# Attention in pairs: two 64-feature heads, or two score maps, placed side by side in the halves of the matmul array

## The chip, the core and the metric

The kernel is one program on one core of a Trainium2 chip. Its time is the device time of one execution in microseconds (us); the figure for the kernel before is the median of three runs. Five engines run their own instruction queues: TensorE (PE) multiplies, with a row of its own for the loading of weights (PEld); VectorE (DVE), ScalarE (ACT) and GpSimd (POOL) work on tiles in the on-chip memory; SyncE (SP) issues the transfers.

## What is computed

Two transformer blocks on 256 tokens of 1024 features, in fp32. The parts that matter here are the attentions. In the first block three of them read the same normalised input, and their outputs go through gated branches that are added up:

```python
# MoBA: 8 heads of 64; with 256 tokens and blocks of 256 it is causal attention
s = einsum('bhqd,bhkd->bhqk', q, k) * 64 ** -0.5;  p = softmax(where(causal, s, -inf));  o = p @ v
# FoX: 8 heads of 64; cum is the running sum of a log-forget gate per head
s = einsum('bhqd,bhkd->bhqk', q, k) * scale + cum_q[..., None] - cum_k[None, :];  then as above
# memory: 4 heads of 128 over 256 memory tokens, not causal
```

The second block has a recurrent mixer and, in its second layer, differential attention: 8 heads of 128, each with two score maps of 64 features,

```python
p = masked_softmax(einsum('bhcqd,bhckd->bhcqk', q, k) * 64 ** -0.5, mask)   # c = 0, 1
attn = p[:, :, 0] - lmb * p[:, :, 1];   o = attn @ v
```

followed by a mixture of 8 experts, of which each token uses 2.

## The kernel before

**Dense work.** All large weights come as items of 1 MB (128 x 2048 fp32) through SP's queue into a ring of buffers (class `Stream`, L217). ACT rounds each item to a high part (L307), DVE subtracts it to get the low part (L309), and PE makes each product in three passes, high by high, high by low and low by high (`mm3`, L477, lines 482, 484 or 486, and 491 or 493). `fm_unit` (L537) makes 128 features by 256 tokens with 24 matmuls; `tok_cols` (L552) makes 128 tokens by 512 features with 24.

**Attention beside it.** Attention is cut into steps that wait in a list called `beside`. `tick()` (L518) takes the next one, and the dense functions call it at fixed places: `fm_unit` behind every 24 matmuls, `tok_cols` in the middle and at the end of 24. So PE's program reads: a dense piece, a step of attention, a dense piece, and so on. Instructions in `urgent()` get a higher priority; within these rules a scheduler puts each engine's instructions in order when the program is built. Each engine runs its queue in that order.

**One step** (`attention`, L793). In step i of 11, for 8 heads and LAG = 2, three things stand in a row: `weigh(i-3)` multiplies the transposed probabilities `pt` by the values `v` into a bank `yp` (L822, L823); `turn(i-2)` transposes the three 128 x 128 blocks of P on PE (L808 to L810) and ACT copies them into `pt`; `begin(i)` calls `scores` (L771). There the first query tile, which sees 128 keys, and the second, which sees 256, each get their query by key product (L781), in FoX the bias as one more product (L783), and on the last 128 keys the causal mask, as a product of the identity with a mask in bf16 (L785). Each tile is an accumulation of its own in one bank of PSUM. Then DVE takes the row's maximum (L788), ACT the exponential with its sum (L789), DVE the reciprocal and the scaling (L790, L803).

A head of 64 features uses half of the array: heads 2j and 2j+1 lie on partitions 0 to 63 and 64 to 127 of the same q and k tile (`pair`, L844), so their score products use different rows of the array; in `weigh` they fill different halves of the output columns. Before the change the two heads of a pair come one step apart.

**Three kinds of this attention.** MoBA's steps lie beside the dense work of `branch(yc)` and the projections for FoX; FoX's lie beside `branch(ym)`. FoX needs two more tiles per head, fq and fk, which DVE makes (`fox_bias`, L898). Differential attention has a `begin` of its own (L1253), which calls `scores` once for each map of a head, with banks from the pools `pa` and `pb` (four PSUM banks each), a `turn` (L1266) and a `step` (L1279); it lies beside the projections of the second half of the heads, whose rotation DVE computes. The memory attention (4 heads of 128 features) goes through the same function with one head in a step.

Of the kernel before, what the change touches and what calls it, by code (L numbers as in the profile page):

```python
# [10 lines left out]
F32 = mybir.dt.float32  # L11
F32R = mybir.dt.float32r
# [3 lines left out]
AF = mybir.ActivationFunctionType  # L16
ALU = mybir.AluOpType
AX = mybir.AxisListType
# [3 lines left out]
S = 256  # L22
# [8 lines left out]
LAG, PRIO = 2, 400  # L31
# [319 lines left out]
def tile_kernel(ctx: ExitStack, tc: tile.TileContext, cst, par, wst, x, mem, g_mix, g_mem, g_ffn, w_forget,  # L351
                moe_w_router, ln_g, ln_b, out):
    nc = tc.nc
    V, A, T = nc.vector, nc.scalar, nc.tensor
# [8 lines left out]
    sm = pool("sm", 2)  # L363
# [16 lines left out]
    f1 = c1.enter_context(tc.tile_pool(name="f1", bufs=1))  # L380
# [34 lines left out]
    ident = cs[:, C_ID:C_ID + 128]  # L415
# [46 lines left out]
    def evac_split(hi, lo, ps):  # L462
        A.activation(out=hi, in_=ps, func=AF.Copy)
        V.tensor_tensor(lo, ps, hi.bitcast(F32), op=ALU.subtract)  # L464
# [303 lines left out]
            A.activation(out=v[:, t], in_=ps, func=AF.Copy)  # L768
        return v

    def scores(sp, q, k, causal, bank, bias=None, bufs=3):  # L771


        n0 = 128 if causal else S
        ps = bank("sc")[:, 0:n0 + S]
        P = sp.tile([128, 512], F32, name="P", tag="P", bufs=bufs)[:, 0:n0 + S]
        nmx = sm.tile([128, 2], F32, tag="nmx", name="nmx", bufs=4)
        sums = sm.tile([128, 2], F32, tag="sums", name="sums", bufs=4)
        for t, c in ((0, slice(0, n0)), (1, slice(n0, n0 + S))):
            nk = c.stop - c.start  # L780
            T.matmul(ps[:, c], q[:, t * 128:t * 128 + 128], k[:, 0:nk], start=True, stop=not causal and bias is None)  # L781
            if bias is not None:
                T.matmul(ps[:, c], bias[0][:, t * 128:t * 128 + 128], bias[1][:, 0:nk], start=False, stop=not causal)  # L783
            if causal:
                T.matmul(ps[:, c.stop - 128:c.stop], identb, causb, start=False, stop=True)  # L785
        with urgent():
            for t, c in ((0, slice(0, n0)), (1, slice(n0, n0 + S))):
                V.tensor_reduce(out=nmx[:, t:t + 1], in_=ps[:, c], axis=AX.X, op=ALU.max, negate=True)  # L788
                A.activation(out=P[:, c], in_=ps[:, c], func=AF.Exp, bias=nmx[:, t:t + 1], accum_out=sums[:, t:t + 1])  # L789
            V.reciprocal(out=sums, in_=sums)  # L790
        return P, sums

    def attention(Y, nh, dh, q, k, v, causal, bias=None):  # L793

        hb = 128 // dh
        n0 = 128 if causal else S
        halves = ((0, slice(0, n0)), (1, slice(n0, n0 + S)))
        P, pt, yp = {}, {}, None

        def begin(h):  # L800
            P[h], rs = scores(f1, q(h), k(h), causal, pa, bias(h) if bias is not None else None)
            for t, c in halves:
                V.tensor_scalar(out=P[h][:, c], in0=P[h][:, c], scalar1=rs[:, t:t + 1], scalar2=None, op0=ALU.mult)  # L803

        def turn(h):
            p = P.pop(h)
            pT = pb("pT").rearrange("p (c t) -> p c t", c=4)
            T.transpose(pT[:, 0], p[:, 0:128], ident)  # L808
            T.transpose(pT[:, 1], p[:, n0:n0 + 128], ident)
            T.transpose(pT[:, 2], p[:, n0 + 128:n0 + 256], ident)  # L810
            if not causal:
                T.transpose(pT[:, 3], p[:, 128:256], ident)
            pt[h] = f1.tile([128, 4, 128], F32, tag="pt", name="pt", bufs=2)
            n = 3 if causal else 4
            A.activation(out=pt[h][:, 0:n], in_=pT[:, 0:n], func=AF.Copy)

        def weigh(h, yp):
            r = h % (2 * hb)
            o = yp[(h % hb) * dh:(h % hb) * dh + dh, r // hb]
            hv = slice(h * dh, h * dh + dh)  # L820
            p = pt.pop(h)
            T.matmul(o, v[:, 0, hv], p[:, 0:2], start=True, stop=False)  # L822
            T.matmul(o[:, 128:256], v[:, 1, hv], p[:, 2], start=False, stop=causal)  # L823
            if not causal:
                T.matmul(o[:, 0:128], v[:, 1, hv], p[:, 3], start=False, stop=True)
            if r == 2 * hb - 1:
                b2 = h // hb - 1
                evac_split(Y[0][:, b2:b2 + 2], Y[1][:, b2:b2 + 2], yp)

        def step(i):  # L830
            nonlocal yp
            h = i - LAG - 1
            if h >= 0:
                if h % (2 * hb) == 0:
                    yp = half(pb("yp"))
                weigh(h, yp)
            if 0 <= i - LAG < nh:
                turn(i - LAG)
            if i < nh:
                begin(i)  # L840

        beside.extend(lambda i=i: step(i) for i in range(nh + LAG + 1))

    def pair(t):  # L844
        return lambda h: t[64 * (h % 2):64 * (h % 2) + 64, h // 2]
# [51 lines left out]

    def fox_bias(h):  # L898
        m = C_MISC
        fq = f1.tile([80, S], F32R, name="fq", tag="fq", bufs=1)  # L900
        fk = f1.tile([80, S], F32R, name="fk", tag="fk", bufs=1)
# [351 lines left out]
    def begin(h):  # L1253
        q, k = qk[h // 4]
        b = h % 4
        P0, r0 = scores(da, q[0:64, b], k[0:64, b], True, pa, bufs=4)
        P1, r1 = scores(da, q[64:128, b], k[64:128, b], True, pb, bufs=4)
        with urgent():
            V.tensor_scalar(out=r1, in0=r1, scalar1=nl, scalar2=None, op0=ALU.mult)
            for t, c in ((0, slice(0, 128)), (1, slice(128, 384))):  # L1260
                V.tensor_scalar(out=P1[:, c], in0=P1[:, c], scalar1=r1[:, t:t + 1], scalar2=None, op0=ALU.mult)
                V.scalar_tensor_tensor(out=P0[:, c], in0=P0[:, c], scalar=r0[:, t:t + 1], in1=P1[:, c],
                                       op0=ALU.mult, op1=ALU.add)
        P[h] = P0
# [507 lines left out]
```

## Time and profile before

| | |
|---|---|
| median of three runs | 1852.12 us (1851.49 to 1852.97) |
| the profiled execution | 1851.57 us; its span 1849.3 us |
| PE busy | 1809.3 us, 98%, 11150 instructions |
| weight loads (PEld) | 1443.3 us, 78% |
| DVE busy | 1107.7 us, 60%, 1609 instructions |
| ACT busy | 874.0 us, 47%, 1224 instructions |
| transfers | 512.70 MB, 277 GB/s over the span |

The span is from the first to the last instruction of the profiled execution. An engine's busy time counts overlapping instructions once. PE's ends are modelled, so a busy PE still may lose time between two shapes of matmul; that is read from the distances of the starts.

### The profile page before, as it was taken

How to read it: one execution, taken by the hardware profiler on the slowest of the kernel's cores; microseconds unless marked ns; L12 is line 12 of the kernel's file. 1: busy time of each engine (PE TensorE's matmuls, PEld its weight loads, DVE VectorE, ACT ScalarE, POOL GpSimd, SP SyncE). 2: the span in 40 equal slices, each digit the busy share in tenths (PEclk: the TensorE clock that was granted, in tenths of full speed). 3: DMA queues.
4: the chain of work that ended last, by engine and by line, in shares of the span. 5: the costliest groups of instructions: out<-in, count | busy, mean ns of one | idle time of the engine just before them, and what ended most of it. 6: DMA issues, size and time to landing. Idle time of an engine off the chain costs nothing.

```text
span 1849.3 us, 27608 instructions
## 1 busy us (share of the span) xinstructions
PE 1809.3 (98%) x11150; PEld 1443.3 (78%) x11150; DVE 1107.7 (60%) x1609; ACT 874.0 (47%) x1224; POOL 0.2 (0%) x4
## 2 busy tenths in 40 slices
PE   8999999999999999999999999999999999999996
PEld 7888898999899899987787767766777676766662
DVE  7756556554577765467779654664656554654522
ACT  6655565444433354435546444553444444553520
POOL 0000000000000000000000000000000000000000
PEclk9999999999999999999999999999999999999998
DMA  7534344655443555544356799999999999999995
GB/s 263 180 117 157 115 160 171 221 189 203 146 159 135 201 198 195 200 165 159 117 227 237 285 389 420 419 419 420 419 419 419 419 419 420 419 419 419 410 419 220
DMA packets 73287, 512.70 MB, mean 277 GB/s; under 512 B 8512, under 2 KB 9152, under 8 KB 12096
## 3 DMA queue, kind: packets, MB, share of 16 engines
q1 hardware_dynamic: 73152, 510.86, 69.9%
q8 instruction: 89, 1.46, 0.3%
q14 instruction: 46, 0.38, 0.1%
HBM read 509.78 MB, written 1.05 MB: 276 GB/s over the span
## 4 chain that ended last, share of the span: by engine, by line
PE 83%; DMA 9%; DVE 6%; ACT 1%; issue 1%; SPq 0%; DVEq 0%; ACTq 0%
DMA wr<-in_wst_dram 8%; PE gu L1593 8%; PE fm L482 7%; PE fm L493 7%; PE fm L486 7%; PE gu L482 5%; PE gu L484 5%; PE gu L491 5%; PE dn L1617 4%; DVE wl L309 3%; PE tk L482 3%; PE tk L484 3%; PE acc L484 3%; PE tk L491 3%; PE acc L482 3%; PE acc L491 3%
## 5 line engine op out<-in xcount | busy, mean ns | idle before, releaser
L309 DVE TENSOR_TENSOR wl<-wr,wh 128x1024 fp32r<-128x1024 f32 x620 | 729.7, 1219 | 355.4 <-ACT wh L307 340.5
L307 ACT ACTIVATE wh<-wr 128x1024 fp32r<-128x1024 f32 x620 | 617.6, 1051 | 297.6 <-issue 84.4
L482 PE MATMUL fm<-xh,wh 128*128 128x256 f32 x1056 | 251.2, 280 | 0.0
L486 PE MATMUL fm<-xl,wh 128*128 128x256 f32 x1056 | 249.4, 278 | 0.0
L1593 PE MATMUL gu<-wr,xfew 128*64 128x256 f32 x1792 | 207.9, 385 | 0.0
L482 PEld LDWEIGHTS fm<-xh,wh 128*128 128x128 f32 x1056 | 198.8, 188 | 1.1 <-issue 0.2
L486 PEld LDWEIGHTS fm<-xl,wh 128*128 128x128 f32 x1056 | 198.6, 188 | 0.9
L1593 PEld LDWEIGHTS gu<-wr,xfew 128*64 128x64 f32 x1792 | 124.8, 138 | 77.4 <-issue 21.1
L482 PE MATMUL gu<-wh,xe 128*128 128x512 f32 (+1 forms) x448 | 177.7, 398 | 0.0
L484 PE MATMUL gu<-wh,xe 128*128 128x512 f32 (+1 forms) x448 | 173.0, 388 | 0.0
L493 PE MATMUL fm<-xh,wl 128*128 128x256 f32 x1056 | 145.4, 278 | 0.0
L493 PEld LDWEIGHTS fm<-xh,wl 128*128 128x128 f32 x1056 | 131.5, 188 | 0.0
L491 PE MATMUL gu<-wl,xe 128*128 128x512 f32 (+1 forms) x448 | 119.3, 388 | 0.4 <-DVE wl L309 0.4
L482 PE MATMUL tk<-wh,xh 128*128 128x512 f32 x288 | 116.6, 405 | 1.7 <-ACT wh L307 1.5
L484 PE MATMUL tk<-wh,xl 128*128 128x512 f32 x288 | 114.5, 397 | 0.4 <-DVE xl L464 0.4
L482 PEld LDWEIGHTS gu<-wh,xe 128*128 128x128 f32 x448 | 84.2, 188 | 31.6 <-ACT wh L307 13.0
L1581 ACT ACTIVATE uf<-uT 128x256 f32<-128x256 f32 x28 | 10.8, 384 | 204.6 <-PE uT L1579 204.6
L1617 PE MATMUL dn<-wr,uf 128*64 128x512 f32 x448 | 103.1, 594 | 2.8 <-ACT uf L1581 1.4
L491 PEld LDWEIGHTS gu<-wl,xe 128*128 128x128 f32 x448 | 83.0, 188 | 19.0 <-DVE wl L309 1.1
L484 PEld LDWEIGHTS gu<-wh,xe 128*128 128x128 f32 x448 | 84.2, 188 | 16.5 <-DVE xe L464 0.3
L482 PE MATMUL dn<-wh,uh 128*128 128x512 f32 x224 | 89.2, 398 | 0.0
L484 PE MATMUL dn<-wh,ul 128*128 128x512 f32 x224 | 88.0, 393 | 0.0
(348 smaller groups left out, 2281.9 us busy)
## 6 DMA issues: line engine op xcount, KB each, us to landing
wr<-in_wst_dram SPq DMA_DIRECT2D x477, 1024.0 KB, 11.8
gb<-in_ln_g_dram SPq DMA_DIRECT2D x3, 512.0 KB, 5.7
gb<-in_ln_b_dram SPq DMA_DIRECT2D x3, 512.0 KB, 6.5
memt<-in_mem_dram SPq DMA_DIRECT2D x2, 512.0 KB, 6.9
res<-in_x_dram SPq DMA_DIRECT2D x2, 512.0 KB, 12.7
wr<-in_wst_dram SPq DMA_DIRECT2D x4, 256.0 KB, 15.6
out_dram<-wr SPq DMA_DIRECT2D x4, 256.0 KB, 3.1
gb<-in_g_mem_dram SPq DMA_DIRECT2D x1, 512.0 KB, 5.3
```

The costliest lines, as they stand in the source:

```text
L307: self.nc.scalar.activation(out=h[:, c], in_=t[:, c], func=AF.Copy)
L309: return [lambda c=c: self.nc.vector.tensor_tensor(l[:, c], t[:, c], h[:, c].bitcast(F32), op=ALU.subtract) for c in cols]
L482: T.matmul(ps, ah, bh, start=first and i == 0, stop=False)
L484: T.matmul(ps, al, bh, start=False, stop=False)
L486: T.matmul(ps, ah, bl, start=False, stop=False)
L491: T.matmul(ps, ah, bl, start=False, stop=last and i == n - 1)
L493: T.matmul(ps, al, bh, start=False, stop=last and i == n - 1)
L1581: A.activation(out=U, in_=pT, func=AF.Copy)
L1593: T.matmul(ps[h, g], xfew[:, u + k, i * FEW:i * FEW + FEW], w[:, k, 256 * b:256 * b + 256], start=u + k == 0, stop=u + k == KD - 1)
L1617: T.matmul(acc[h], U[:, j, b * FEW:b * FEW + FEW], wd[n][:, k], start=c == 1 and k == 0, stop=end and k == 3)
```

## The change

`scores` takes a list of heads and a bank for each. It issues all query by key products first, tile by tile and in each tile head by head, then all biases, then all causal masks. In each bank both query tiles are one accumulation: the start flag stands on the first tile alone, and the stop flag on the last mask. Two heads of 64 features (or the two maps of one head of differential attention) are made in one call.

`attention` works on groups of hb = 128 // dh heads: two of 64 features, one of 128. For two, `weigh` alternates the two heads, and the list `beside` gets `begin(g)` and `after(g)` (weighing and transposing) as separate entries: 4 groups to begin and 5 to follow, 9 entries in place of 11 steps. P has four buffers instead of three, fq and fk two instead of one.

```diff
-    def scores(sp, q, k, causal, bank, bias=None, bufs=3):
+    def scores(sp, heads, causal, banks, bufs=4):
...
-        for t, c in ((0, slice(0, n0)), (1, slice(n0, n0 + S))):
-            nk = c.stop - c.start
-            T.matmul(ps[:, c], q[:, t * 128:t * 128 + 128], k[:, 0:nk], start=True, stop=not causal and bias is None)
-            if bias is not None:
-                T.matmul(ps[:, c], bias[0][:, t * 128:t * 128 + 128], bias[1][:, 0:nk], start=False, stop=not causal)
-            if causal:
-                T.matmul(ps[:, c.stop - 128:c.stop], identb, causb, start=False, stop=True)
+        halves = ((0, slice(0, n0)), (1, slice(n0, n0 + S)))
+        pss = [bank("sc")[:, 0:n0 + S] for bank in banks]
+        out = []
+        for t, c in halves:
+            for ps, (q, k, bias) in zip(pss, heads):
+                T.matmul(ps[:, c], q[:, t * 128:t * 128 + 128], k[:, 0:c.stop - c.start], start=t == 0 or not causal,
+                         stop=not causal)
...
+        if causal:
+            for t, c in halves:
+                for ps in pss:
+                    T.matmul(ps[:, c.stop - 128:c.stop], identb, causb, start=False, stop=t == 1)
...
-        def weigh(h, yp):
...
+        def weigh(g):
+            nonlocal yp
+            if g % 2 == 0:
+                yp = half(pb("yp"))
+            hs = [(yp[j * dh:j * dh + dh, g % 2], slice((g * hb + j) * dh, (g * hb + j + 1) * dh), pt.pop(g * hb + j))
+                  for j in range(hb)]
+            for o, hv, p in hs:
+                T.matmul(o, v[:, 0, hv], p[:, 0:2], start=True, stop=False)
+            for o, hv, p in hs:
+                T.matmul(o[:, 128:256], v[:, 1, hv], p[:, 2], start=False, stop=causal)
...
-        beside.extend(lambda i=i: step(i) for i in range(nh + LAG + 1))
+        if hb == 1:
+            beside.extend(lambda i=i: step(i) for i in range(n + lag + 1))
+        else:
+            for i in range(n + lag + 1):
+                if i < n:
+                    beside.append(lambda i=i: begin(i))
+                if i >= lag:
+                    beside.append(lambda i=i: after(i))
...
-        P0, r0 = scores(da, q[0:64, b], k[0:64, b], True, pa, bufs=4)
-        P1, r1 = scores(da, q[64:128, b], k[64:128, b], True, pb, bufs=4)
+        (P0, r0), (P1, r1) = scores(da, [(q[r, b], k[r, b], None) for r in (slice(0, 64), slice(64, 128))], True, (pa, pb))
```

On PE, in MoBA's stretch, one step of one head stood between two dense pieces before (`yp` the weighted values, `pT` the transposed probabilities, `sc` the scores, `fm` dense work; a number is the place in PE's program):

```order
537 L822 MATMUL yp<-pt,v 64x256
538 L823 MATMUL yp<-pt,v 64x128
539 L808 MATMUL pT<-cs,P 128x128
540 L809 MATMUL pT<-cs,P 128x128
541 L810 MATMUL pT<-cs,P 128x128
542 L781 MATMUL sc<-qk 128x128
543 L785 LDWEIGHTS identb
544 L785 MATMUL sc<-causb,identb 128x128
545 L781 MATMUL sc<-qk 128x256
546 L785 LDWEIGHTS identb
547 L785 MATMUL sc<-causb,identb 128x128
548 L482 MATMUL fm<-xh,wh 128x256
```

After the change one entry holds the scores of two heads:

```order
566 L781 MATMUL sc<-qk 128x128 x2
567 L781 MATMUL sc<-qk 128x256 x2
568 L791 LDWEIGHTS identb
569 L791 MATMUL sc<-causb,identb 128x128
570 L791 LDWEIGHTS identb
571 L791 MATMUL sc<-causb,identb 128x128
572 L791 LDWEIGHTS identb
573 L791 MATMUL sc<-causb,identb 128x128
574 L791 LDWEIGHTS identb
575 L791 MATMUL sc<-causb,identb 128x128
576 L482 MATMUL fm<-xh,wh 128x256
```

Another entry, behind a dense piece of its own, holds the weighing of one pair and the transposes of the next:

```order
593 L840 MATMUL yp<-pt,v 64x256 x2
594 L842 MATMUL yp<-pt,v 64x128 x2
595 L824 MATMUL pT<-cs,P 128x128
596 L825 MATMUL pT<-cs,P 128x128
597 L826 MATMUL pT<-cs,P 128x128
598 L824 MATMUL pT<-cs,P 128x128
599 L825 MATMUL pT<-cs,P 128x128
600 L826 MATMUL pT<-cs,P 128x128
601 L482 MATMUL fm<-xh,wh 128x256
```

The same instructions stand in PE's program for two heads, in two interruptions of the dense work as before; the masks have moved behind all four products, and products of the two heads alternate.

On DVE, in the same stretch, the softmax of one head stood in a row before (`nmx` the negated maximum, `sums` the sums of the exponentials, `P` the probabilities, `wl` the low part of dense weights):

```order
162 L309 TENSOR_TENSOR wl<-wr,wh 128x1024 x2
163 L788 TENSOR_REDUCE nmx<-sc 128x1 x2
164 L790 RECIPROCAL sums<-sums 128x2
165 L803 TENSOR_SCALAR P<-P,sums 128x128
166 L803 TENSOR_SCALAR P<-P,sums 128x256
167 L788 TENSOR_REDUCE nmx<-sc 128x1 x2
```

After the change that of two heads does, with the maxima of both first:

```order
164 L309 TENSOR_TENSOR wl<-wr,wh 128x1024 x2
165 L798 TENSOR_REDUCE nmx<-sc 128x1 x4
166 L801 RECIPROCAL sums<-sums 128x2
167 L818 TENSOR_SCALAR P<-P,sums 128x128
168 L818 TENSOR_SCALAR P<-P,sums 128x256
169 L801 RECIPROCAL sums<-sums 128x2
170 L818 TENSOR_SCALAR P<-P,sums 128x128
171 L818 TENSOR_SCALAR P<-P,sums 128x256
172 L309 TENSOR_TENSOR wl<-wr,wh 128x1024 x2
```

The second head's maxima have moved ahead of the first head's reciprocal; nothing else lies between.

## Rows read from the trace of the kernel before

**Rows 1.** The page: the chain that ended last, shares by engine.

```profile
PE 83%; DMA 9%; DVE 6%; ACT 1%; issue 1%; SPq 0%; DVEq 0%; ACTq 0%
```

**Rows 2.** Stretches: length; busy us of PE, PEld, DVE, ACT, POOL; clock; DMA share; GB/s.

```profile
99.00:149.00 50.00, 50.00 (x354) 40.94 (x352) 27.89 (x57) 29.85 (x59) 0.00 (x0) 1.00 0.36 129
192.00:245.00 53.00, 53.00 (x368) 43.61 (x367) 33.21 (x72) 29.51 (x59) 0.00 (x0) 1.00 0.32 120
861.00:926.00 65.00, 65.00 (x312) 46.86 (x311) 46.96 (x120) 34.71 (x92) 0.00 (x0) 1.00 0.34 124
1080.00:1410.00 330.00, 328.48 (x1870) 235.11 (x1868) 186.97 (x192) 154.09 (x189) 0.00 (x0) 1.00 1.01 419
```

**Rows 3.** Timeline of PE, one step of MoBA: start us, us, engine, line, operation.

```profile
117.45 1.07 PE L493 MATMUL fm<-xh,wl 128*128 128x256 f32 x8
118.45 0.65 PE L822 MATMUL yp<-pt,v 128*64 128x256 f32 x2
118.94 0.38 PE L823 MATMUL yp<-pt,v 128*64 128x128 f32 x2
119.25 0.33 PE L808 MATMUL pT<-cs,P 128*128 128x128 f32 x1
...
119.73 0.48 PE L781 MATMUL sc<-qk 64*128 64x128 f32 x2
120.14 0.23 PE L785 MATMUL sc<-causb,identb 128*128 128x128 bf16 x1
120.30 0.70 PE L781 MATMUL sc<-qk 64*128 64x256 f32 x2
120.93 0.23 PE L785 MATMUL sc<-causb,identb 128*128 128x128 bf16 x1
120.97 0.36 PE L482 MATMUL fm<-xh,wh 128*128 128x256 f32 x1
121.17 0.28 PE L486 MATMUL fm<-xl,wh 128*128 128x256 f32 x1
```

**Rows 4.** Timeline of PE: matmuls on half of the array, in four windows.

```profile
1125.96 0.44 PE L1593 MATMUL gu<-wr,xfew 128*64 128x256 f32 x2
...
1265.60 1.12 PE L1627 MATMUL sp<-ye,PU 64*128 64x512 f32 x2
...
1832.10 0.70 PE L1627 MATMUL sum<-ye,PU 64*128 64x512 f32 x2 [0.81 <-ACT ye L1622]
...
1832.10 1.99 PE L1627 MATMUL sum<-ye,PU 64*128 64x512 f32 x8 [0.81 <-ACT ye L1622]
```

**Rows 5.** Timeline of PE: scores of a FoX head, and the dense matmul behind.

```profile
197.26 0.48 PE L781 MATMUL sc<-qk 64*128 64x128 f32 x2
...
198.90 0.37 PE L482 MATMUL fm<-xh,wh 128*128 128x256 f32 x1
```

**Rows 6.** Timeline of PE: both maps of one head of differential attention.

```profile
903.73 0.48 PE L781 MATMUL sc<-dq 64*128 64x128 f32 x2
...
906.34 0.48 PE L482 MATMUL tk<-wh,xh 128*128 128x512 f32 x1
```

**Rows 7.** Timeline of DVE: softmax of one head, first and last.

```profile
101.43 0.29 DVE L788 TENSOR_REDUCE nmx<-sc 128x1 f32<-128x128 f32 x1 [0.26 <-PE sc L785]
...
103.51 0.55 DVE L803 TENSOR_SCALAR P<-P,sums 128x128 f32<-128x128 f32 x2
```

**Rows 8.** Timeline: a rotation's last addition and the transposes that read it.

```profile
897.65 0.68 DVE L1194 TENSOR_TENSOR ra<-ra,rb 128x512 f32<-128x512 f32 x1
...
898.48 0.63 PE L739 MATMUL tp<-cs,ra 128*128 128x128 f32 x4
```

**Rows 9.** Waits of DVE, 861 to 926 us: us in total, times, longest.

```profile
DVE nmx L788 <- PE sc L785: 8.7, 12, 1.1
...
DVE wl L309 <- PE tk L491: 1.1, 2, 0.7
DVE ra L1189 <- PE tk L491: 0.8, 2, 0.4
```

**Rows 10.** Stretch just behind a pause of PE, columns as in rows 2.

```profile
839.30:842.80 3.50, 3.50 (x9) 2.73 (x10) 3.25 (x4) 3.50 (x5) 0.00 (x0) 0.51 0.89 248
```

More of the change, by code (lines that the diff above doesn't have):

```diff
@@ L769, in val @@
         return v
-    def scores(sp, q, k, causal, bank, bias=None, bufs=3):
+    def scores(sp, heads, causal, banks, bufs=4):
         n0 = 128 if causal else S
[L775 to L778, printed above, removed]
-        for t, c in ((0, slice(0, n0)), (1, slice(n0, n0 + S))):
-            nk = c.stop - c.start
-            T.matmul(ps[:, c], q[:, t * 128:t * 128 + 128], k[:, 0:nk], start=True, stop=not causal and bias is None)
-            if bias is not None:
-                T.matmul(ps[:, c], bias[0][:, t * 128:t * 128 + 128], bias[1][:, 0:nk], start=False, stop=not causal)
-            if causal:
-                T.matmul(ps[:, c.stop - 128:c.stop], identb, causb, start=False, stop=True)
-        with urgent():
[L787 to L791, printed above, removed]
@@ new lines, in scores @@
+        halves = ((0, slice(0, n0)), (1, slice(n0, n0 + S)))
[6 more added lines that the diff above has]
+        for t, c in halves:
+            for ps, (q, k, bias) in zip(pss, heads):
+                if bias is not None:
+                    T.matmul(ps[:, c], bias[0][:, t * 128:t * 128 + 128], bias[1][:, 0:c.stop - c.start], start=False,
+                             stop=False)
@@ new lines, in scores @@
+        if causal:
+            for t, c in halves:
+                for ps in pss:
+                    T.matmul(ps[:, c.stop - 128:c.stop], identb, causb, start=False, stop=t == 1)
+        with urgent():
+            for ps in pss:
+                P = sp.tile([128, 512], F32, name="P", tag="P", bufs=bufs)[:, 0:n0 + S]
+                nmx = sm.tile([128, 2], F32, tag="nmx", name="nmx", bufs=4)
+                sums = sm.tile([128, 2], F32, tag="sums", name="sums", bufs=4)
+                for t, c in halves:
+                    V.tensor_reduce(out=nmx[:, t:t + 1], in_=ps[:, c], axis=AX.X, op=ALU.max, negate=True)
+                    A.activation(out=P[:, c], in_=ps[:, c], func=AF.Exp, bias=nmx[:, t:t + 1],
+                                 accum_out=sums[:, t:t + 1])
+                V.reciprocal(out=sums, in_=sums)
+                out.append((P, sums))
@@ L793, in attention @@
+        return out
     def attention(Y, nh, dh, q, k, v, causal, bias=None):
@@ L798, in attention @@
         P, pt, yp = {}, {}, None
[L800 to L810, printed above, removed]
-            if not causal:
[L812 to L815, printed above, removed]
@@ L817, in weigh @@
-        def weigh(h, yp):
[L818 to L828, printed above, removed]
@@ L830, in step, with begin @@
-        def step(i):
[L831 to L839, printed above, removed]
-                begin(i)
-        beside.extend(lambda i=i: step(i) for i in range(nh + LAG + 1))
+        def begin(g):
+            hs = range(g * hb, g * hb + hb)
+            made = scores(f1, [(q(h), k(h), bias(h) if bias is not None else None) for h in hs], causal, (pa, pb)[0:hb])
+            for h, (p, rs) in zip(hs, made):
+                P[h] = p
+                for t, c in halves:
+                    V.tensor_scalar(out=p[:, c], in0=p[:, c], scalar1=rs[:, t:t + 1], scalar2=None, op0=ALU.mult)
@@ new lines, in turn @@
+        def turn(g):
+            for h in range(g * hb, g * hb + hb):
+                p = P.pop(h)
+                pT = pb("pT").rearrange("p (c t) -> p c t", c=4)
+                T.transpose(pT[:, 0], p[:, 0:128], ident)
+                T.transpose(pT[:, 1], p[:, n0:n0 + 128], ident)
+                T.transpose(pT[:, 2], p[:, n0 + 128:n0 + 256], ident)
+                if not causal:
+                    T.transpose(pT[:, 3], p[:, 128:256], ident)
+                pt[h] = f1.tile([128, 4, 128], F32, tag="pt", name="pt", bufs=2)
+                n = 3 if causal else 4
+                A.activation(out=pt[h][:, 0:n], in_=pT[:, 0:n], func=AF.Copy)
@@ new lines, in weigh @@
+        def weigh(g):
[8 more added lines that the diff above has]
+                T.matmul(o[:, 128:256], v[:, 1, hv], p[:, 2], start=False, stop=causal)
+            if not causal:
+                for o, hv, p in hs:
+                    T.matmul(o[:, 0:128], v[:, 1, hv], p[:, 3], start=False, stop=True)
+            if g % 2:
+                evac_split(Y[0][:, g - 1:g + 1], Y[1][:, g - 1:g + 1], yp)
@@ new lines, in attention, with after @@
+        n = nh // hb
+        lag = LAG // hb
+        def after(i):
+            if i - lag - 1 >= 0:
+                weigh(i - lag - 1)
+            if 0 <= i - lag < n:
+                turn(i - lag)
+        def step(i):
+            after(i)
+            if i < n:
+                begin(i)
+        if hb == 1:
+            beside.extend(lambda i=i: step(i) for i in range(n + lag + 1))
+        else:
+            for i in range(n + lag + 1):
+                if i < n:
+                    beside.append(lambda i=i: begin(i))
+                if i >= lag:
+                    beside.append(lambda i=i: after(i))
@@ L899, in fox_bias @@
         m = C_MISC
-        fq = f1.tile([80, S], F32R, name="fq", tag="fq", bufs=1)
-        fk = f1.tile([80, S], F32R, name="fk", tag="fk", bufs=1)
+        fq = f1.tile([80, S], F32R, name="fq", tag="fq", bufs=2)
+        fk = f1.tile([80, S], F32R, name="fk", tag="fk", bufs=2)
         src = parts.bitcast(F32)
```

## The prediction

> **What bounds the kernel now.** Read first the chain of work that ended last [rows 1]: 83% of the span lies on TensorE (PE), 9% on transfers, 6% on VectorE (DVE). A shorter PE program therefore pays, if the stretch that it leaves is PE's and if what follows moves with it. So read next the busy time by stretch [rows 2]: in the three stretches with attention that the change touches (first kind 99 to 149 us, second 192 to 245, third 861 to 926) PE is busy for the whole of each (50.00 of 50, 53.00 of 53, 65.00 of 65), while DVE has 27.89, 33.21 and 46.96 and the DMA engines a share of 0.32 to 0.36. In the fourth row, the experts, the transfers are full instead (share 1.01, 419 GB/s). That stage is fed from buffers that earlier PE work frees, and before it the transfers are a third busy, so it starts earlier by what the stages before it lose, and I carry the gain through at 1 to 1.
>
> Then look into one step on PE [rows 3]. Dense matmuls follow each other every 0.113 us (eight in 1.07, the last taking 0.28). The step of one head stands between 118.45 and 120.97: weighing 0.80 (two passes each of L822 and L823), three transposes 0.48, scores 1.24, in all 2.52. At its front the last dense matmul starts at 117.45 + 7 x 0.113 = 118.24, its successor was due at 118.35 and L822 starts at 118.45: 0.10 lost. Behind it L482 and L486 stand 0.20 apart instead of 0.11: 0.09 lost.
>
> **What a piece is made of.** Scores: the first query tile (128 keys) takes 119.73 to 120.14, 0.41, the second (256 keys) 120.30 to 120.93, 0.63. Each is two passes, so 128 columns more in both cost 0.22, and one pass streams 128 columns in 0.11. Streaming is then 0.22 and 0.44, and 0.19 of each is the first load of weights and the stop before the next shape. The mask (L785) adds 0.16 and 0.04. The sum is 0.66 + 0.38 + 0.20 = 1.24. Weighing has the same 0.66 of streaming and 0.14 around it; the transposes are 3 x 0.11 and a stop of 0.15.
>
> **What the change does to it.** Two heads now stand in a row, one in either half of the array. Whether the halves run side by side is the first thing to settle, and this trace has both kinds. Halves of the output columns: two passes of L1593 over 256 columns take 0.44 in all, two passes of one half (L822, same shape) 0.65 [rows 3, 4]. Halves of the input rows: two passes of L1627 over 512 columns take 1.12 when one half works alone at 1265.60 and 0.70 when both work at 1832.10, and eight take 1.99 where the lone rate would be about 1.12 + 6 x 0.43 = 3.7 [rows 4]. So I take it that both halves stream at once.
>
> Scores of two heads: 0.66 of streaming once, 0.19 once, since the mask no longer stands between the tiles, and four masks behind one another at about 0.05 (one pass of 128 columns in a narrower type; the 0.16 before held one of them and a stop of 0.10): 1.05 for 2.48, which saves 1.43. If the halves don't overlap, 1.71 and 0.77.
> Weighing: 0.80 for both heads, saves 0.80; without overlap 1.46, saves 0.14.
> Transposes: 6 x 0.11 and a load of 0.05, with dense matmuls of the same shape behind them and so no stop: 0.71 for 0.96, saves 0.25.
> Ends: two interruptions for two heads as before, but only that with scores has the 0.09 behind it: saves 0.09.
> Sum for a pair: 2.57 with overlap, 1.25 without.
>
> First kind: four pairs, 10.3 us (5.0 without overlap). Second kind: its scores take 197.26 to 198.90, 1.64 [rows 5], 0.40 more than the first kind's, for two passes with the bias; four such passes in a row at 0.11 and some loading, 0.50, replace 0.80: 0.30 more for each pair (bounds 0 and 0.36), 11.5 us (5.0). Third kind: two maps of a head take 903.73 to 906.34, 2.61 [rows 6], and will take 1.05: 1.56 for each of eight heads, 12.5 us (7.2 at 1.71). PE's program is shorter by 34.3 us, or by 17.2 without overlap.
>
> The single accumulation of both tiles changes flags and no instruction: nothing. The second fq and fk and the fourth P cost memory alone. No DMA is issued or removed; loads on SP's queue follow the buffers as before.
>
> **What is late next.** In the first two kinds a group's transposes stand two dense pieces or more behind its scores. The softmax of one head takes 101.43 to 104.06, 2.63 us [rows 7]; that of two interleaves on DVE and ScalarE, I estimate about 4. Two pieces of 24 matmuls at 0.113 are 5.4, and the interleaved group or transposes add 0.7 to 1.5. That covers it, even with one pair of weight subtractions in between. The fourth head's fk stands behind the first head's reciprocal in the second kind; it is ready about when its pass comes. For all such small waits I take 1 us off.
>
> The third kind is tighter. DVE is busy for 46.96 of 65 there and partly beside PE's own chain: its addition at 897.65 ends at 898.33, and the transposes that read it start on PE at 898.48, as soon as the last dense matmul is through [rows 8]. With PE earlier, DVE decides there. What it can give back is what it now waits for PE: 8.7 + 1.1 + 0.8 = 10.6 us [rows 9]; the short wait that each of eight heads keeps for its first scores, about 0.2, leaves 9.0. So I take 9.0 of the 12.5 (from 6, where half the waits return for ScalarE's results, to 12.5).
>
> The sum: 10.3 + 11.5 + 9.0 - 1.0 = 29.8. The profiled execution took 1851.57 us, 2.3 of it outside the span of 1849.3, and stands 0.55 below the median of 1852.12. From the median that gives 1822.3.
>
> **Rivals.**
> 1. Halves that start in strict order. Head A's second pass would have to start before head B's first. Tile for tile the streaming of a group, scores as well as weighing, then takes 0.88 instead of 0.66 (the last pass of either head stands alone). That is 0.44 for each of eight pairs and up to 0.22 for each head of the third kind, 3.5 to 5.3 in all: about 1826. Against it: the two passes at 1832.10 end within 0.70 where one pass of that length takes nearly all of it, so they started together [rows 4]. The Trainium skill ("TensorE: Matmul & The Clock Gate", section "Part 3: Packing small matmuls — row/col tiling") says that matmuls keep strict program order in start and end; it would speak for 1826. The trace doesn't bear it out for the two passes of one fp32 matmul, so it gets 8%.
> 2. No overlap at all: 17.2 saved on PE, and the third kind's 7.2 is less than DVE can follow; with 1 off, 1836. For it speaks only that no score matmuls of two halves are neighbours in this trace. 6%.
> 3. DVE takes more of the third kind, and of the second, where fq and fk of two heads now come at once: gain 6 there and 3 less before, 23.8: 1828. For it: DVE's 46.96 of 65 and ScalarE's results, for which it waits too. 13%.
> 4. The gain doesn't reach the end, because the expert stage's transfers set the time from a start of their own. Then nothing is saved: 1852. Against it: the share of 0.34 in the third stretch shows that they wait for buffers that PE and DVE free. 2%.
> 5. Slower: each group's transposes wait on PE for the two heads' softmax, and the waits pull down the clock. There is a place in this trace where PE paused and then ran at 0.51, the lower of the two levels (1.2 GHz, for 2.4), for 3.5 us [rows 10], which costs 1.75. Eight pairs and eight heads make 16 such places; with 34.3 to gain, it takes over 2.1 us at each to lose, and with 1.75 and a wait of 1.5 each the time is 1852.1 - 34.3 + 52 = 1870. Against it: the cover of 6 us and more computed above, where a softmax of two heads would have to take over 8. 3%.
>
> **How the numbers follow.** The forecast of 1822 has 68%; its own range, from 1816 (all 34.3, and the 1.75 of the clock at its lower level gone) to 1826. The rivals at 1826 and 1828 lie close above it, that at 1836 outside. The range 1815 to 1833 holds the forecast and rivals 1 and 3. A measurement of this kernel can tell 0.2%, 3.7 us, from no change; all cases but 4 and 5 are faster by more: 0.95, with 0.02 for no change and 0.03 for slower.
>
> **What would show it.** In the first kind's groups: scores of two heads from first pass to the next dense matmul in 1.0 to 1.2 us, eight passes with starts in twos; 1.7 means rival 2, 1.3 rival 1. Weighing and transposes together in about 1.5. PE without idle time in the first two stretches, which end some 10 and 22 us earlier; idle PE before L1297 or the rotation's transposes in the third would show DVE as its bound. The experts' stretch should have the same length and share of transfers as before, and only start earlier. A first stretch that shrinks by less than 7 us would make the prediction wrong.

## The result, and the profile after

The changed kernel takes 1820.58 us (median of four runs, 1820.11 to 1823.63) where the kernel before takes 1851.80 beside it (1851.44 to 1852.97): a ratio of 0.9834, 95% interval 0.9817 to 0.9851, 31.2 us less. The forecast was 1822 (its sum 1822.3), with a range from 1815 to 1833.

The shares of the chain that ended last, by engine, moved little from [rows 1]:

```profile
PE 79%; DMA 11%; DVE 7%; ACT 2%; issue 1%; SPq 0%; DVEq 0%; ACTq 0%
```

The same stretches of work as in [rows 2], found by the same dense matmuls, with the same columns:

```profile
98.70:138.70 40.00, 40.00 (x355) 36.40 (x354) 26.30 (x57) 28.04 (x59) 0.00 (x0) 1.00 0.43 159
181.60:224.10 42.50, 42.50 (x369) 38.69 (x368) 30.10 (x70) 28.15 (x59) 0.00 (x0) 1.00 0.41 150
838.70:893.80 55.10, 54.43 (x310) 40.98 (x309) 45.85 (x120) 33.20 (x92) 0.00 (x0) 1.00 0.40 139
1048.00:1378.00 330.00, 328.49 (x1868) 234.96 (x1866) 187.96 (x193) 155.15 (x189) 0.00 (x0) 1.00 1.01 419
```

The three stretches are about 10 us shorter each. PE is still busy for all of the first two; in the third it now has 0.67 us of idle time, and DVE is busy for 83% of it (45.85 of 55.10) where it was for 72% (46.96 of 65.00). The experts' stretch is what it was (328.49 busy of 330, transfers full) and only starts earlier.

PE's program has the same 7272 dense matmuls in both kernels, so a stage is best measured by how much earlier a certain one of them starts. Counted along the program, from 0:

| dense matmul | starts before | after | earlier by | of it in this stage |
|---|---|---|---|---|
| 288, ahead of the first kind | 97.05 | 96.90 | 0.15 | |
| 576, behind it | 151.94 | 141.57 | 10.37 | 10.22 |
| 1016, behind the second kind | 245.97 | 225.00 | 20.97 | 10.60 |
| 4800, in the layer of the third kind, ahead of its attention | 838.41 | 817.87 | 20.55 | -0.42 |
| 4824, ahead of the third kind | 846.11 | 823.98 | 22.12 | 1.57 (clock, below) |
| 5064, behind it | 934.02 | 901.86 | 32.17 | 10.05 |
| 7264, near the end | 1784.13 | 1754.33 | 29.80 | -2.37 (1.7 of it between 972.8 and 982, the clock) |

PE in the first kind's stretch, to be read beside [rows 3]: the scores of a pair, a dense piece, then weighing and transposes.

```profile
111.19 0.93 PE L781 MATMUL sc<-qk 64*128 64x128 f32 x8
112.05 0.40 PE L791 MATMUL sc<-causb,identb 128*128 128x128 bf16 x4
112.26 0.36 PE L482 MATMUL fm<-xh,wh 128*128 128x256 f32 x1
...
114.18 1.07 PE L493 MATMUL fm<-xh,wl 128*128 128x256 f32 x8
115.18 0.65 PE L840 MATMUL yp<-pt,v 128*64 128x256 f32 x4
115.66 0.39 PE L842 MATMUL yp<-pt,v 128*64 128x128 f32 x4
115.98 0.33 PE L824 MATMUL pT<-cs,P 128*128 128x128 f32 x1
...
116.61 0.37 PE L482 MATMUL fm<-xh,wh 128*128 128x256 f32 x1
```

Eight passes of scores take 0.86 to the first mask; one after the other they would stream 4 x 0.11 + 4 x 0.22 = 1.32. Four passes of weighing start and end as two did before (0.65). From the first pass of scores to the next dense matmul it is 1.07, from weighing to the next dense matmul 1.43.

In the second kind, beside [rows 5], four products with the bias take 0.57:

```profile
182.36 0.93 PE L781 MATMUL sc<-qk 64*128 64x128 f32 x8
183.22 0.73 PE L786 MATMUL sc<-fk,fq 80*128 80x128 f32 x4
183.79 0.40 PE L791 MATMUL sc<-causb,identb 128*128 128x128 bf16 x4
183.99 0.36 PE L482 MATMUL fm<-xh,wh 128*128 128x256 f32 x1
```

In the third, beside [rows 8], PE now waits for the rotation's addition:

```profile
857.95 0.68 DVE L1222 TENSOR_TENSOR ra<-ra,rb 128x512 f32<-128x512 f32 x1
...
858.77 0.63 PE L739 MATMUL tp<-cs,ra 128*128 128x128 f32 x4 [0.42 <-DVE ra L1222]
```

And of what DVE waited there for PE's scores, 8.7 us in [rows 9], 2.7 are left (839 to 903 us). Its wait for ScalarE's sums stays as it was (3.5 us before, 861 to 926 us):

```profile
DVE sums L801 <- ACT P L799: 3.7, 4, 1.5
DVE nmx L798 <- PE sc L791: 2.7, 2, 2.2
```

### The profile page after: what moved, and what is told of

The parts are those of the page before. It is cut to its first block, busy times and chain, and to the rows that moved or that the text cites. A ratio compares the mean times of both kernels' runs of the same rounds, so it can differ in the third digit from the quotient of the medians.

```text
span 1818.6 us, 27621 instructions
## 1 busy us (share of the span) xinstructions
PE 1777.8 (98%) x11150; PEld 1427.3 (78%) x11150; DVE 1103.4 (61%) x1609; ACT 867.8 (48%) x1222; POOL 0.2 (0%) x4
## 3 DMA queue, kind: packets, MB, share of 16 engines
HBM read 509.78 MB, written 1.05 MB: 281 GB/s over the span
## 4 chain that ended last, share of the span: by engine, by line
PE 79%; DMA 11%; DVE 7%; ACT 2%; issue 1%; SPq 0%; DVEq 0%; ACTq 0%
DMA wr<-in_wst_dram 10%; PE gu L1620 8%; PE fm L482 7%; PE fm L493 7%; PE fm L486 7%; PE gu L482 5%; PE gu L484 5%; PE gu L491 5%; PE dn L1644 4%; PE acc L484 3%; PE acc L482 3%; PE acc L491 3%; DVE wl L309 3%; PE tk L484 3%; PE tk L482 3%; PE tk L491 3%
```

## The experiments

All are compared by the dense matmuls of the table: gain of the first, second and third kind against the trace of before. The changed kernel has 10.22, 10.60 and 10.05; its second trace gave 10.21, 10.61 and 10.06, and the second trace of before 0.00 three times, so a hundredth or two is the resolution of this measure, while the total times of one kernel spread over 1 to 5 us.

| run | median us (range) | first | second | third |
|---|---|---|---|---|
| changed kernel | 1820.58 (1820.11 to 1823.63) | 10.22 | 10.60 | 10.05 |
| same half | 1830.91 (1829.57 to 1831.69) | 5.04 | 5.45 | 10.00 |
| head by head | 1821.26 (1820.87 to 1826.24) | 10.14 | 10.55 | 10.07 |
| masks between | 1825.56 (1821.80 to 1827.05) | 8.68 | 9.58 | 9.40 |
| the same, two starts | 1825.85 (1824.84 to 1827.15) | 8.68 | 9.60 | 9.36 |
| third as before | 1830.16 (1828.35 to 1832.36) | 10.21 | 10.61 | -0.06 |
| one entry | 1824.22 (1822.28 to 1826.00) | 8.77 | 8.11 | 10.00 |
| third, less on VectorE | (stage only) | 10.21 | 10.61 | 11.30 |
| third, scaling on ScalarE | 1822.21 (1821.74 to 1822.87) | 10.21 | 10.61 | 9.75 |
| third, scaling on GpSimd | 1828.99 (1827.85 to 1833.26) | 10.21 | 10.61 | 1.59 |

My theory: the two halves of the array stream at once, which gives about half of the gain of the first two kinds (in the prediction's sum a pair saves 2.57 with overlap and 1.25 without); fewer changes of shape give the rest; VectorE takes back part of it in the third kind. The rival that matters most: the gain comes from the regrouping, wherever the heads sit.

**Both heads of a pair in the same half.**

```diff
+        def heads_of(g):
+            return (4 * (g // 2) + g % 2, 4 * (g // 2) + g % 2 + 2) if hb == 2 else (g,)
...
-            hs = range(g * hb, g * hb + hb)
+            hs = heads_of(g)
...
```

> The changed kernel, but in the first two kinds heads 0 and 2, 1 and 3, 4 and 6, 5 and 7 make the pairs, so both heads of a pair sit in the same half of the array (weighing goes head by head). Number and size of all instructions stay. Theory A (two halves stream at once; a pair's streaming of 0.66 us is paid once): without it the 0.66 is paid twice for scores and twice for weighing. Scores of a pair go from 1.27 to 1.93 us between dense matmuls, weighing with transposes from 1.64 to 2.30, 8 pairs lose 8 x 1.32 = 10.6: 1831. Theory B (the gain comes from fewer changes of shape between matmuls, wherever the heads sit): no change, 1820.6. If only one of the two kinds of half (rows or columns) overlaps: 1826. The third kind keeps its gain in all of them.

```profile
112.13 1.57 PE L781 MATMUL sc<-qk 64*128 64x128 f32 x8
113.64 0.40 PE L791 MATMUL sc<-causb,identb 128*128 128x128 bf16 x4
...
116.76 0.65 PE L843 MATMUL yp<-pt,v 128*64 128x256 f32 x2
117.24 0.38 PE L844 MATMUL yp<-pt,v 128*64 128x128 f32 x2
117.46 0.59 PE L843 MATMUL yp<-pt,v 128*64 128x256 f32 x2
117.89 0.38 PE L844 MATMUL yp<-pt,v 128*64 128x128 f32 x2
118.20 0.33 PE L827 MATMUL pT<-cs,P 128*128 128x128 f32 x1
```

The same eight passes of scores take 1.51 to the first mask instead of 0.86, and weighing 1.44 to the transposes instead of 0.80. The two kinds lose 5.18 and 5.15, where theory A said 5.28 each. Half of their gain is overlap of halves, of rows (0.65 for the scores of a pair) and of columns (0.64 for the weighing) alike; the other half is the regrouping and stays. It is 5.04 and 5.45, where the prediction's sum without overlap had 5.0 for either kind.

**All of one head ahead of the other.**

```diff
-        for t, c in halves:
-            for ps, (q, k, bias) in zip(pss, heads):
+        for ps, (q, k, bias) in zip(pss, heads):
+            for t, c in halves:
                 T.matmul(ps[:, c], q[:, t * 128:t * 128 + 128], k[:, 0:c.stop - c.start], start=t == 0 or not causal,
...
                 T.matmul(o, v[:, 0, hv], p[:, 0:2], start=True, stop=False)
-            for o, hv, p in hs:
                 T.matmul(o[:, 128:256], v[:, 1, hv], p[:, 2], start=False, stop=causal)
```

> The changed kernel, but within a pair all products of the first head stand ahead of those of the second, for scores (all three kinds) and weighing; masks and biases stay behind. Pairs still sit in different halves. Theory A1 (halves overlap, but matmuls start in the order of the program): the second head's first pass can start only with the first head's last. Scores then stream 1.10 instead of 0.66 us, weighing 1.21 instead of 0.66: 0.99 for each of 8 pairs and 0.44 for each of 8 heads of the third kind (less there, as VectorE hides part): 8 to 11 slower, 1829 to 1832. Theory A2 (each half has its own queue): no change, 1820.6. Theory A3 (only neighbours in strict alternation overlap at all): 0.66 for each, 13 to 16 slower, 1834 to 1837.

```profile
112.71 0.93 PE L781 MATMUL sc<-qk 64*128 64x128 f32 x8
113.58 0.40 PE L791 MATMUL sc<-causb,identb 128*128 128x128 bf16 x4
...
112.71 0.39 PE L781 MATMUL sc<-qk 64*128 64x128 f32 x2
...
116.70 0.66 PE L840 MATMUL yp<-pt,v 128*64 128x256 f32 x4
```

Next to nothing changes: 0.87 to the first mask, weighing 0.66 for four passes, and the two kinds gain 0.08 and 0.05 less. The third line is a window of 30 ns from 112.70, and two passes start in it. In the program as it is written, the instruction behind head A's first product is head A's second; two passes of one head that start 0.11 apart end after 0.48 [rows 3], these after 0.39, so the other one is head B's, past the rest of head A. The order of the built program isn't shown for this run, but the starts show that it changed: wherever eight passes of scores or four of weighing stand together, B's first pass now starts 13 or 14 ns behind A's, and 6 or 7 ns in the changed kernel. In these rows each half takes its own next work; the sentence that each engine runs its queue in order holds for the starts on PE within a half only. The order in which the change interleaves the heads is not what makes them overlap. Theory A2 stands, A1 and A3 fall.

**The masks between the tiles.** The masks (and biases) of a tile move into the loop behind its products:

```diff
-        for t, c in halves:
             for ps, (q, k, bias) in zip(pss, heads):
                 if bias is not None:
...
-        if causal:
-            for t, c in halves:
+            if causal:
                 for ps in pss:
```

> The changed kernel, but the masks (and in the second kind the biases) of the first query tile stand right behind its two products, ahead of the second tile's products. Same instructions. The sum of the prediction counts 0.19 us for each return from a mask to a half-array product (first load of weights and the stop before the next shape), once for each call of scores: 16 x 0.19 = 3.0, of which the third kind's half may be hidden by VectorE: 1822 to 1824; scores of a pair in the first kind 1.46 instead of 1.27. Rival: the gain is all from the two halves, and grouping the masks is worth nothing: 1820.6.

```profile
111.64 0.49 PE L781 MATMUL sc<-qk 64*128 64x128 f32 x4
112.07 0.28 PE L789 MATMUL sc<-causb,identb 128*128 128x128 bf16 x2
112.28 0.70 PE L781 MATMUL sc<-qk 64*128 64x256 f32 x4
112.92 0.28 PE L789 MATMUL sc<-causb,identb 128*128 128x128 bf16 x2
113.01 0.36 PE L482 MATMUL fm<-xh,wh 128*128 128x256 f32 x1
```

Scores of a pair go from 1.07 to 1.37 (0.30 more; 0.36 in the second kind, 0.30 for a head of the third). Grouping the masks is worth more than the 0.19 that I had, because the expectation counted the first load of weights alone; the stop of 0.10 behind a mask, which the prediction had read beside it in [rows 3], comes on top. The stages lose 1.54, 1.02 and 0.65. Of the 1.54, 1.2 are the masks, and 0.3 are dense matmuls that follow each other a little more slowly (in four pieces at 0.118 instead of 0.113); of the second kind the masks take 1.4, and its dense matmuls give 0.4 back. For these distances, which differ from program to program and repeat in the second traces, I have no cause. In the third kind six heads are 0.30 longer, 1.83 in all; the first head of each half, which dense matmuls divide, isn't (0.14 shorter together). The changed kernel's waits for VectorE, worth 1.04 (below), are gone, and 0.65 is left. Of the total time, 5.0 us above the changed kernel's, these 3.2 are what the stages show; its runs spread over 5.

**Two accumulations in a bank.** As the run before, with start on the first product of both tiles:

```diff
-                T.matmul(ps[:, c], q[:, t * 128:t * 128 + 128], k[:, 0:c.stop - c.start], start=t == 0 or not causal,
+                T.matmul(ps[:, c], q[:, t * 128:t * 128 + 128], k[:, 0:c.stop - c.start], start=True,
...
-                    T.matmul(ps[:, c.stop - 128:c.stop], identb, causb, start=False, stop=t == 1)
+                    T.matmul(ps[:, c.stop - 128:c.stop], identb, causb, start=False, stop=True)
```

> As the run with the masks between, but each query tile of a bank is again an accumulation of its own (start on its first product, stop on its mask). It differs from that run by flags alone. Theory: flags cost nothing; scores of a pair in the first kind stay at 1.57 us between dense matmuls, in the second at 2.20, and the stages end where they did (the last dense matmul ahead of the second block's output projection within 0.3 of 904.6). Rival: a start flag costs something of its own (a stop of 0.05 to 0.10 for the second tile): 16 x 0.1 = 1.6 more.

```profile
112.15 0.49 PE L781 MATMUL sc<-qk 64*128 64x128 f32 x4
112.57 0.28 PE L789 MATMUL sc<-causb,identb 128*128 128x128 bf16 x2
...
113.52 0.36 PE L482 MATMUL fm<-xh,wh 128*128 128x256 f32 x1
```

1.37 again, and the same gains by stage. The flags cost nothing. The end lies 1.1 later than I had named, as the run was 0.5 later from its start and 0.6 more between the second and the third kind, where the two kernels don't differ. Two open accumulations in one bank, with all masks at the end, weren't tried.

**The third kind as before.**

```diff
...
-        (P0, r0), (P1, r1) = scores(da, [(q[r, b], k[r, b], None) for r in (slice(0, 64), slice(64, 128))], True, (pa, pb))
+        P0, r0 = scores_one(da, q[0:64, b], k[0:64, b], True, pa, bufs=4)
+        P1, r1 = scores_one(da, q[64:128, b], k[64:128, b], True, pb, bufs=4)
```

> The changed kernel, but the third kind's two maps are made by two calls of the old scores function, as before the change. If the stages add up, the time is what the first two kinds alone bring. The traces put 10.1 us on the third kind: 1830.6. If VectorE's share had been as I forecast (9.0): 1829.6. If the third kind's PE savings came through whole (12.5): 1833. If the gain of a stage were lost or regained further on by when its work meets transfers: off these by more than 2.

The other two keep 10.21 and 10.61, the third is at -0.06: the stages add up, and 1830.16 is what the sum says (1830.6).

**Weighing, transposes and scores in one entry.**

```diff
-        if hb == 1:
+        if True:
             beside.extend(lambda i=i: step(i) for i in range(n + lag + 1))
```

> The changed kernel, but weighing, transposes and scores of a group stand in one entry of the list (as for the heads of 128), so there are 6 entries in place of 9 for each of the first two kinds. Theory: three interruptions fewer save the 0.10 ahead of each and some of the first loads, 0.2 x 3 for each kind; but a group's transposes now stand one dense piece (2.7 us) and the weighing (0.8) behind its scores, where its softmax took about 4 us from the last mask at 205.7 to the last scaling at 209.7: PE waits 0 to 1 us for each of 8 groups. 1819.5 to 1827, likeliest 1822, with PE waiting ahead of the transposes. Rival: the softmax is early enough, and the time falls to 1819.4.

PE in the second kind's stretch; the idle time ahead of the second head's transposes is a wait as expected:

```profile
194.89 0.39 PE L842 MATMUL yp<-pt,v 128*64 128x128 f32 x4
...
196.17 0.30 PE L824 MATMUL pT<-cs,P 128*128 128x128 f32 x1 [0.89 <-DVE sums L801]
196.40 0.49 PE L781 MATMUL sc<-qk 64*128 64x128 f32 x2
...
196.82 0.33 PE L825 MATMUL pT<-cs,P 128*128 128x128 f32 x1
```

1.45 and 2.49 us are lost. This wait of 0.89 us for the softmax is the only one of PE that the trace records between 98 and 240 us. In one group of either kind two passes of the next scores stand between the transposes, with two more changes of shape; in the first kind that entry takes 3.47 us from dense matmul to dense matmul where the next one takes 2.88. Some 0.4 of the 1.45 are again dense matmuls at a greater distance. So the separate entries, with two dense pieces between a group's scores and its transposes, are worth 4 us, but how much of that is waiting and how much the order of PE's program isn't shown.

The additional buffers of the change (P, fq and fk) weren't tried alone. In the trace of before PE has no wait between 99 and 245 us that they could have ended, and the third kind's P had four buffers already.

**Less work on VectorE in the third kind.** The line that scales the second map's probabilities is left out, so the attention has other values:

```diff
-                V.tensor_scalar(out=P1[:, c], in0=P1[:, c], scalar1=r1[:, t:t + 1], scalar2=None, op0=ALU.mult)
```

> The changed kernel without the scaling of the second map's probabilities on VectorE in the third kind (2 instructions for each of 8 heads, 0.54 us; this part of the computation is left out). Theory: VectorE decides part of the third kind: PE's program there is 12.3 shorter than before, the stretch 10.1. With 4.3 us less on VectorE up to 2.3 come back: the third kind ends 1.0 to 2.3 earlier, 1818.3 to 1819.6, and PE's first wait ahead of the rotation's transposes and head 3's (0.6) is gone. Rival: ScalarE or PE itself decides; no change.

Only the stage can be read: the experts' work depends on the data, and here it went on to 2905 us. The third kind gains 11.30, 1.25 more. PE's waits ahead of the rotation's and of a later head's transposes are gone, and VectorE waits for PE again, for scores and for buffers of low parts that PE still reads (839 to 903 us):

```profile
DVE nmx L798 <- PE sc L791: 3.3, 4, 1.5
DVE wl L309 <- PE tk L491: 3.2, 2, 2.6
```

So VectorE did decide part of this stage. Of the 1.25, 0.73 lie at these two waits. The other 0.51 lie at the first head of the second half, where the scheduler, with this line gone, puts the first products of the two maps together again; in the changed kernel they stand apart, and don't overlap:

```profile
871.25 0.49 PE L781 MATMUL sc<-dq 64*128 64x128 f32 x2
...
872.77 0.48 PE L781 MATMUL sc<-dq 64*128 64x128 f32 x2
```

**That scaling on another engine.** `A.activation(out=P1[:, c], in_=P1[:, c], func=AF.Copy, scale=r1[:, t:t + 1])` in its place, or the same operation as `nc.gpsimd.tensor_scalar`:

> As the changed kernel, but the scaling of the second map's probabilities in the third kind is made by ScalarE (2 activations for each of 8 heads, about 0.37 and 0.47 us, 6.7 in all). VectorE has 4.3 less, ScalarE, busy for 39.8 of 64 us there, 6.7 more. If VectorE decides and ScalarE has room: 1819 to 1820.5. Rival: VectorE waits for ScalarE's results already (3.7 us for the sums), and a longer chain there makes the third kind later: 1821 to 1824.

> As the changed kernel, but the scaling of the second map's probabilities in the third kind is made by GpSimd, which has nothing else to do (2 instructions for each of 8 heads). Leaving this work out moved the third kind by 1.3 us, so that is the most to be had: 1819.3, if GpSimd takes about as long as VectorE (0.54 for two). Rival: GpSimd is slower by some factor (no row shows this operation on it), and the chain from scores to transposes gets longer by more than it frees: at 1 us more for each head the third kind ends later by the share of 8 that PE can't cover, 1821 to 1825.

ScalarE gives 9.75 in place of 10.05: nothing won. VectorE now waits for its scaling (2.2 us in four waits, 839 to 903 us), and PE's transposes for VectorE (1.1 us). GpSimd gives 1.59. Its instructions and the waits behind them (839 to 915 us for PE's):

```profile
L1288 POOL TENSOR_SCALAR P<-P,sums 128x128 f32<-128x128 f32 (+1 forms) x16 | 13.0, 825 | 886.7 <-DVE sums L1286 862.8 <-ACT v L1017 13.9 <-DVE nmx L798 5.0
```

```profile
PE pT L1297 <- DVE P L1289: 6.1, 10, 1.4
PE tp L739 <- DVE ra L1222: 1.7, 1, 1.7
```

The two of a head take 1.50 us in seven of the eight heads (825 ns in the mean of all 16), where VectorE needs 0.54 for both, and the longer chain from scores to transposes costs 8.5 us of the stage; the time of 1828.99 lies above the 1825 that I had given that rival at most. No version tried that computes the same is faster than the changed kernel.

**The clock, from two traces of each kernel.**

> The kernel before once more, for a second trace. In its first trace PE's clock was down from 838.4 to 842.6 us, in that of the changed kernel from 972.8 to 976.5. If these pauses belong to the kernels' timing, they come again at these places; if they fall differently from one execution to the next, one or both are missing or elsewhere, and some 1.5 us of the difference between any two traces is not the change's.

> The changed kernel once more, for a second trace and times beside the next run. Interruptions of the dense work as in its first trace (1.27 and 1.64 in the first kind, to 0.01); the third kind gives 10.0 to 10.1; the end within 2 us of 1820.6.

The changed kernel's second trace has the same interruptions (gains 10.21, 10.61, 10.06; median 1821.35, 1819.34 to 1821.69). The clock doesn't repeat. In the second trace of before, with the columns of [rows 2], the last row but one a stretch in which PE mostly waits:

```profile
839.30:842.80 3.50, 3.25 (x14) 2.45 (x14) 3.23 (x4) 3.45 (x5) 0.00 (x0) 1.00 0.88 282
1001.50:1005.50 4.00, 1.46 (x6) 0.59 (x5) 4.00 (x5) 1.79 (x2) 0.00 (x0) 0.88 0.00 0
1006.20:1011.10 4.90, 4.90 (x14) 3.84 (x13) 4.90 (x6) 3.58 (x5) 0.00 (x0) 0.50 0.93 348
```

In the first trace of before the same pause and the stretch behind it, and then, in the changed kernel, the stretch with this work:

```profile
1000.00:1004.00 4.00, 1.82 (x7) 0.66 (x5) 4.00 (x5) 2.21 (x3) 0.00 (x0) 1.00 0.00 0
1006.20:1011.10 4.90, 4.90 (x23) 4.00 (x22) 4.90 (x6) 4.70 (x6) 0.00 (x0) 1.00 0.98 385
```

```profile
972.80:976.50 3.70, 3.70 (x13) 2.92 (x12) 3.70 (x4) 3.09 (x4) 0.00 (x0) 0.62 0.90 303
```

A granted clock of 0.50 is the lower of the two levels, 1.00 the full one, and 0.62 or 0.88 the mean of a stretch that has both. The stretch at 839 had the lower clock in the first trace [rows 10] and the full one in the second; the one at 1006 the other way round. Both stand behind a pause of PE, and whether the clock falls there differs from one execution of the kernel before to the next. The changed kernel's clock fell behind the later of the two pauses in both of its traces. By the same dense matmuls the five falls ahead of 1012 us cost 1.58 us in the first trace of before, 1.54 and 2.78 in the second, 1.71 and 1.28 in the changed kernel's two.

## Why the prediction was right

| term | forecast | measured |
|---|---|---|
| scores of a pair, first kind | 1.43 | 2 x 1.24 - 1.07 = 1.41 |
| weighing and transposes of a pair | 1.05 | 2 x 1.28 - 1.43 = 1.13 |
| ends | 0.09 | 0.00 |
| first kind | 10.3 | 10.22 |
| second kind | 11.5 | 10.60 |
| third kind, on PE / come through | 12.5 / 9.0 | 11.1 / 10.05 |
| small waits | -1.0 | none in the first two kinds |
| sum | 29.8 | 30.9 by stage, 31.2 by the medians |

- **Overlap of halves.** Read from a lone and a shared pair of passes [rows 4], it held for rows and columns, to 2% of the price of taking it away. The small terms of a pair were off by 0.08 and 0.09 with opposite signs: weighing and transposes save more, and the ends nothing, because the dense matmuls behind the transposes are late too (0.21 us from 116.61 to the next one, where 0.11 is usual).
- **Rival 1, strict order,** is refuted harder than I thought. The Trainium skill ("TensorE: Matmul & The Clock Gate", section "Part 3: Packing small matmuls — row/col tiling") has matmuls start and end in program order; here passes of the second head start ahead of the first head's remaining ones, and a kind loses 0.05 to 0.08 us by it, so the measurement decides against that rule for products in different halves.
- **The second kind** came 0.9 short. Four products with the bias take 0.57, not 0.50. In the middle of the chain a pair saves 2 x (3.113 - 0.113) - (1.839 + 1.640 - 0.226) = 2.75 us, from dense matmul to dense matmul, and all interruptions together save 11.1, four times that. The other 0.5 is lost between them. Within a piece the dense matmuls follow each other at either 0.113 or 0.118 us, and of the eleven pieces beside this attention nine have the longer distance after the change and four had it before. No run shows the cause.
- **The third kind** came out 1.05 above its term by two errors of opposite sign. PE's program got 9.27 + 1.17 + 0.66 = 11.1 us shorter and not 12.5. Six heads save 1.54 each. In the first head of each half dense matmuls stand between the two query tiles, and it saves less: 1.17 in the first half, and 0.66 in the second, where the first products of the two maps stand apart as well (871.25 and 872.77 above). What VectorE takes back is 1.04 and not 3.5: 0.62 at the rotation's transposes, and 0.42 at a later head's, the wait for L1297 that the prediction named beside them:

```profile
892.55 0.30 PE L1297 MATMUL pT<-cs,P 128*128 128x128 f32 x1 [0.25 <-DVE P L1289]
```

  So VectorE as the engine that takes the rest was right, its size was not. The 9.0 was what its waits for PE could give back, and they gave back less: 10.6 us in the stretch of [rows 9], 2.7 in that of after. A wait of 1.2 us for ScalarE's rounding is gone too, and VectorE is busy for 1.11 us less with the same 120 instructions, which the prediction didn't count. That the term came near is in part luck.
- **The 1 us of small waits isn't there.** The trace shows no wait of PE between 95 and 230 us. The cover of two dense pieces holds; with one it doesn't always, as the wait of 0.89 us in the run with one entry shows. The misses (-0.9, +1.05, +1.0) have both signs, so the sum is closer than its parts, which is luck.
- **Carried to the end.** The experts' stretch kept its length, and the gain behind the third kind, 32.17, was 29.80 near the end. Most of the difference, like the 1.57 ahead of the third kind, is a clock that fell in one trace and not in the other; I had put such clock losses in the range alone (1.75), which is where they belong. Between the second traces the gain behind the third kind is 31.91 and grows to 39.67 near the end, so what one pair of traces shows behind the third kind is not the change's alone; that the gain comes through at about 1 to 1 rests on the medians (31.2) against the stages (30.9), and on the run with the third kind as before.

## What to carry to other kernels

Two small matmuls that use different halves of the array's rows, or of its columns, cost the time of one, in whatever order they are issued next to each other; look for lone ones, and for pairs that the scheduler has put apart. A change of shape and back costs 0.30 us in this stream, so group products of a shape, and leave two pieces of dense work between scores and what needs their softmax. Measure a stage by the start of the same dense matmul in both traces: that resolves 0.02 us, where total times spread over 1 to 5. Then divide the stage into its interruptions and the dense matmuls between them, for the distance of the latter can change as well.

## What was not expected of the hardware

Each half of the array takes its next work past instructions of the other half that stand ahead of it in the program. The price of going from half-array products to a mask and back is 0.30 us: the 0.19 of the load and the 0.10 of the mask's stop. Whether TensorE's clock falls behind a given pause changes between executions of the kernel before, and each of five falls cost 1.3 to 2.8 us. GpSimd needs nearly three times as long as VectorE to scale two tiles of fp32 (1.50 and 0.54 us).
